# Finer steps for the gate and forget bursts of a decoder block, a step of its own for the head output's transposes, and a later wait for the last branch output

## The chip, the cores and the metric

The kernel runs on one core of a Trainium2 chip. The metric is the device time of one execution in microseconds, lower is better; times are the median of several runs.

## The reference, cut to what matters

One layer of a hybrid decoder over 256 positions of width 2048, in float32. Every weight matrix is read once.

```python
h = rmsnorm(x, g_pre_mix)
proj = h @ w_in                      # 2048 x 15376
aq, ak, av, az, ab, aa, bq, bf, bi, bz, cq, gates = split(proj)
oa = gated_head_norm(gated_deltanet(conv_silu(aq, ak, av), beta, logdecay), az)   # branch A, 8 heads of 128
log_f = logaddexp(log(lb), log1p(-lb) + log_sigmoid(bf))                          # branch B: forget gate
ob = gated_head_norm(hgrn2(silu(bq), log_f, bi), bz)                              # branch B, 8 heads of 128
oc = memory_attention(cq, rmsnorm(mem), w_kv_mem)                                 # branch C, 4 heads of 256
ga, gb, gc = split(sigmoid(gates))
merged = ga * (oa @ w_br_a) + gb * (ob @ w_br_b) + gc * (oc @ w_br_c)
x = x + rmsnorm(merged @ w_out, g_post_mix)
x = x + rmsnorm(square(relu(rmsnorm(x, g_pre_mlp) @ w1)) @ w2, g_post_mlp)        # w1: 2048 x 8192
```

Here gated_head_norm(o, z, g) is o / rms(o) * g * silu(z), per head.

## The kernel before

Every float32 product is made of three: each operand is split into a high part of a narrower type and a low part, and high x high, high x low and low x high are added in PSUM. The weights are split on the fly. A *weight group* is 256 rows x 512 columns of a matrix: one DMA on SP's queue into `w` (512 KB), a cast on ACT into `wh` (the high part), a subtraction on DVE into `wl` (the low part). `w`, `wh` and `wl` have four buffers each, so ACT and DVE can be at most four groups ahead of PE's last use.

A *unit* is one output block of 512 columns. `unit` makes 12 products of 512 columns per group (two k tiles, two row tiles, three products). `unit_joined`, for the projections whose result is wanted with channels on partitions, joins the two activation parts into one wide product (512 columns) and one narrow one (256 columns), 8 of each per group; it runs its 8 groups as pairs, and the first and the last pair in two halves of the output, so that the first half's sum can leave PSUM while the second is made. Its result goes out in two pieces, each a copy on ACT and an add on DVE (`sum<-mm`).

All other work hangs in *steps* between the groups: generators that `yield`, in the list `bg`. After each group `tick` adds the rate (R1 to R4, 1.1 to 1.2) to a credit, and `pump` runs so many steps of the first generator in the list. With `in_place` set, the first instruction of a step on DVE, ACT and PE keeps its place in the written order; the framework's scheduler may move the others by priority and readiness. Each engine then runs its queue strictly in order (PE may load weights ahead). So a step that waits at the head of ACT's or DVE's queue also holds up the casts and subtractions behind it.

The order of the program: memory attention's keys and values; the queries of C; branch A's projections (twice, four heads each), with `gen_a` as steps; branch 2 (C's gates and output); branch B's projections, twice, each time with `forget` (put ahead of all other steps) and `gen_b`; branch 0 (A's), branch 1 (B's); w_out; the MLP. A branch is four times a gate unit (sigmoid into `sg`) and an output unit of four groups, whose result times `sg` is added into `mg`.

- `forget(ps, hg)` makes log-sigmoid values of a projection: on ACT an absolute value, which waits in the place of the table switch, the table load, exp, ln (all into `fe`), then DVE and four more exps into `ft`.
- `gen_b` starts with `bm` and `bd` on DVE, then the same burst (abs, table load, exp, ln) on `bd`, then `kq`, the sum `bm + bd`, and the chunk's decay products (`ad`, `pa`, `bo` on PE).
- `head_out` is the end of `gen_a` and `gen_b`: squares on ACT, a reduction on DVE, a power on POOL (`r`), eight scalings on DVE (`on`), eight transposes on PE (`oT`), split into `oh` and `ol`.
- In `gen_a`, the triangular inverse is built by products `pw` and `pzt`, a masked copy into `XT` on DVE, and transposes `X`.

Of the kernel before, what the change touches and what calls it, by code (L numbers as in the profile page):

```python
# [33 lines left out]
KG = 2  # L34
BL = 16
WB = 4
R1, R2, R3, R4 = 1.1, 1.2, 1.2, 1.2


@with_exitstack  # L40
def tile_trunk(ctx: ExitStack, tc, a):
# [26 lines left out]
    def step_marks(begins):  # L68
        for e in (V, A, T):
            e.step_begins = begins and in_place[0]  # L70
# [14 lines left out]
    def nm(s):  # L85
        cnt[0] += 1
        return f"{s}_{cnt[0]}"

    def g4(name, shape=(P, 1024), dt=F32):
        return gp.tile(list(shape), dt, tag="g", name=nm(name))  # L90
# [5 lines left out]
    def small(name, n=16):  # L96
        if n > 16:
            return sp64.tile([P, 64], F32, tag="s64", name=nm(name))[:, 0:n]
        t = sp.tile([P, 16], F32, tag="s", name=nm(name))
        return t[:, 0:n]  # L100

    def bank(name):
        return pbp.tile([P, 512], F32, tag="bp", name=nm(name))
# [37 lines left out]
    def own_table(ins):  # L141
        other_table[0] = ins.ins
        return ins
# [10 lines left out]
    def pump(n=1):  # L154
        while n > 0 and bg:
            step_marks(True)
            try:
                next(bg[0])
                n -= 1
            except StopIteration:  # L160
                bg.pop(0)
            step_marks(False)

    def drain():
        while bg:
            pump(1)
# [12 lines left out]
    def tick(share=1.0):  # L179
        credit[0] += rate[0] * share  # L180
        n = int(credit[0])
        credit[0] -= n
        pump(n)
# [22 lines left out]
    def load_w(src, k0, n, c0, width=512, home=None):  # L206
        return split_w(load_w_raw(src, k0, n, c0, width), n, width, home=home)

    def unit(act, nk, src, c0, r0=0, order=None, split=False, post=None, ws=None):

        if split:
            ps = [bank("mm") for _ in range(2)]
        else:
            both = pmm.tile([P, 1024], F32, tag="mm", name=nm("mm"))
            ps = [both[:, 0:512], both[:, 512:1024]]
        if order is None:
            order = [(g, None) for g in range(nk // KG)]  # L220
        ws = ws or {}
        for i, (g, tt) in enumerate(order):
            k0 = g * KG
            if g not in ws:
                ws[g] = load_w(src, r0 + k0, KG, c0)
            wh, wl = ws[g]
            for j in range(KG):
                kt = k0 + j
                ah, al = act(kt)
                for t in range(NT) if tt is None else (tt,):  # L230
                    o = ps[t]
                    st, sl = ah[:, t * P:(t + 1) * P], al[:, t * P:(t + 1) * P]
                    T.matmul(o, st, wh[:, j, :], start=kt == 0, stop=False)
                    T.matmul(o, st, wl[:, j, :], start=False, stop=False)
                    T.matmul(o, sl, wh[:, j, :], start=False, stop=kt == nk - 1)
            tick()
            if post is not None and i + 1 in post:
                post[i + 1](ps)
        return ps if split else both
# [56 lines left out]
    def act_of(tiles):  # L296
        return lambda kt: (tiles[kt // 4][0][:, kt % 4, :], tiles[kt // 4][1][:, kt % 4, :])
# [9 lines left out]
    def split_psum(ps, hi, lo):  # L307
        A.copy(hi, ps)
        V.tensor_tensor(out=lo, in0=ps, in1=hi.bitcast(F32), op=ALU.subtract)
# [14 lines left out]
    def rstd_of(ss, n, count):  # L324

        v = small("v", n)
        V.tensor_scalar(out=v, in0=ss, scalar1=1.0 / count, scalar2=EPS, op0=ALU.mult, op1=ALU.add)
        r = small("r", n)
        G.tensor_tensor(out=r, in0=v, in1=mhalf[:, 0:n], op=ALU.pow)  # L329
        return r  # L330
# [409 lines left out]
    oa = [None, None]  # L740
    ob = [None, None]
# [33 lines left out]
    def head_out(o, z, rq, dst, hg):  # L775

        sq = g4("sq", (P, 8, P))
        A.activation(sq, o, AF.Square)
        ss = small("ss", 8)
        V.tensor_reduce(out=ss, in_=sq, axis=AX.X, op=ALU.add)  # L780
        yield
        if rq is not None:
            V.tensor_tensor(out=ss, in0=ss, in1=rq, op=ALU.mult)
            V.tensor_tensor(out=ss, in0=ss, in1=rq, op=ALU.mult)
        sc = rstd_of(ss, 8, P)
        if rq is not None:
            sc2 = small("sc2", 8)
            V.tensor_tensor(out=sc2, in0=sc, in1=rq, op=ALU.mult)
            sc = sc2
        on = g4("on", (P, 8, P))  # L790
        for b in range(8):
            V.scalar_tensor_tensor(out=on[:, b, :], in0=o[:, b, :], scalar=sc[:, b:b + 1], in1=z[:, b, :],
                                   op0=ALU.mult, op1=ALU.mult)
            if b % 4 == 3:
                yield
        hi, lo = g4("oh", (P, 4, S), F32R), g4("ol", (P, 4, S), F32R)
        for hh in range(2):
            pt = bank("oT")
            for q in range(2):
                for t in range(NT):  # L800
                    T.transpose(pt[:, q * S + t * P:q * S + (t + 1) * P], on[:, t * 4 + hh * 2 + q, :], ident)
            split_psum(pt.rearrange("p (q s) -> p q s", q=2), hi[:, hh * 2:hh * 2 + 2, :], lo[:, hh * 2:hh * 2 + 2, :])
        yield
        dst[hg] = (hi, lo)
# [262 lines left out]
    def gen_merge(j):  # L1067
        if j == 3:
            yield
            yield  # L1070
        hi, lo = g4("mgh", (P, 4, S), F32R), g4("mgl", (P, 4, S), F32R)
        for hh in range(2):
            pt = bank("mgT")
            for q in range(2):
                for t in range(NT):
                    c = hh * 2 + q
                    T.transpose(pt[:, q * S + t * P:q * S + (t + 1) * P], mg[j][:, t, c * P:(c + 1) * P], ident)
            split_psum(pt.rearrange("p (q s) -> p q s", q=2), hi[:, hh * 2:hh * 2 + 2, :], lo[:, hh * 2:hh * 2 + 2, :])
        mgs[j] = (hi, lo)
        yield  # L1080

    def branch(gi, o, w_br):
        oact = act_of(o)
        for j in range(4):
            ps = unit(hact, KT, w_in, OFF_G + gi * D + 512 * j)
            sg = g4("sg", (P, NT, 512))
            own_table(A.activation(sg, ps.rearrange("p (t n) -> p t n", t=NT), AF.Sigmoid))
            ps = unit(oact, 8, w_br, 512 * j).rearrange("p (t n) -> p t n", t=NT)
            if gi == 2:
                mg[j] = g4("mg", (P, NT, 512))  # L1090
                V.tensor_tensor(out=mg[j], in0=ps, in1=sg, op=ALU.mult)
            else:
                V.tensor_tensor(out=sg, in0=ps, in1=sg, op=ALU.mult)
                V.tensor_tensor(out=mg[j], in0=mg[j], in1=sg, op=ALU.add)
            if gi == 1:
                bg.append(gen_merge(j))
# [4 lines left out]
    def forget(ps, hg):  # L1101

        t, g = g4("ft", (P, 4, S)), g4("fg", (P, 4, S))

        def steps():
            e = g4("fe", (P, 4, S))
            exp_ln_table(e, ps)
            pin(A.activation(e, e, AF.Exp, scale=-1.0))
            pin(A.activation(e, e, AF.Ln, bias=1.0))
            yield  # L1110
            yield
            V.scalar_tensor_tensor(out=t, in0=ps, scalar=0.0, in1=e, op0=ALU.max, op1=ALU.add)
            yield
            for h in range(4):
                c = hg * 4 + h
                A.activation(t[:, h, :], t[:, h, :], AF.Exp, scale=-1.0, bias=lbl1[:, c:c + 1])
            V.scalar_tensor_tensor(out=g, in0=ps, scalar=0.0, in1=e, op0=ALU.min, op1=ALU.subtract)
            yield

        ahead_of_all(steps())  # L1120
        return t, g

    def gen_b(hg, k, g, q, v, z):
# [9 lines left out]
                yield  # L1133
        exp_ln_table(d, d)
        pin(A.activation(d, d, AF.Exp, scale=-1.0))
        pin(A.activation(d, d, AF.Ln, bias=1.0))
        kq, kqh, kql = g4("kq"), g4("kqdh", dt=F32R), g4("kqdl", dt=F32R)
        V.tensor_tensor(out=kq, in0=k.rearrange("p h s -> p (h s)"), in1=q.rearrange("p h s -> p (h s)"), op=ALU.mult)
# [118 lines left out]
        o = g4("ob", (P, 8, P))  # L1257
# [20 lines left out]
        bg.append(gen_b(hg, k, g, q, v, z))  # L1278
    rate[0] = R4

    while oa[1] is None:
        pump(1)
    branch(0, oa, a["w_br_a"][0])
    drain()


    def load_gbc(src):
        r = []
        for c in range(2):
            t = g4("gbc")  # L1290
            adma(t, src[0:1, c * 1024:(c + 1) * 1024].to_broadcast([P, 1024]))
            r.append(t)
        return r

    gbc = load_gbc(a["g_post_mix"])
    branch(1, ob, a["w_br_b"][0])

    def gb(c):
        return gbc[c // 2][:, c % 2 * 512:c % 2 * 512 + 512]
# [210 lines left out]
```

## Time and profile before

| what | value |
|---|---|
| median of three runs | 1805.83 us (1805.63 to 1806.97) |
| the profiled execution | 1805.44 us |
| its span, first to last instruction | 1803.7 us |
| PE busy | 1787.2 us, 99% |
| DVE busy | 1152.7 us, 64% |
| ACT busy | 901.8 us, 50% |
| mean granted PE clock | 0.997 |
| HBM read | 332.75 MB, 186 GB/s over the span |

The profile is of one execution. Its engines are PE (matmuls), PEld (PE's weight loads), DVE, ACT, POOL and SP. All instructions that go through the kernel's recording helper have line 56, so rows are told apart by the names of the tiles, output first (`wl<-w,wh`). In a timeline row the first number is the start in us, the second the length, and a bracket gives the engine's idle time before it and what ended that. The ends of matmuls are modelled; a stream of them is read by its starts.

### The profile page before, as it was taken

How to read it: one execution, taken by the hardware profiler on the slowest of the kernel's cores; microseconds unless marked ns; L12 is line 12 of the kernel's file. 1: busy time of each engine (PE TensorE's matmuls, PEld its weight loads, DVE VectorE, ACT ScalarE, POOL GpSimd, SP SyncE). 2: the span in 40 equal slices, each digit the busy share in tenths (PEclk: the TensorE clock that was granted, in tenths of full speed). 3: DMA queues.
4: the chain of work that ended last, by engine and by line, in shares of the span. 5: the costliest groups of instructions: out<-in, count | busy, mean ns of one | idle time of the engine just before them, and what ended most of it. 6: DMA issues, size and time to landing. Idle time of an engine off the chain costs nothing.

```text
span 1803.7 us, 23759 instructions
## 1 busy us (share of the span) xinstructions
PE 1787.2 (99%) x9137; PEld 1522.9 (84%) x9137; DVE 1152.7 (64%) x1599; ACT 901.8 (50%) x1148; POOL 59.7 (3%) x100
## 2 busy tenths in 40 slices
PE   9999999999999999999999999999999999999998
PEld 7888888888888888888788888888888888888886
DVE  6865768684867577696555557555655565655556
ACT  6645566454554464555444445544444444444433
POOL 0000000400120000000000000000000000000000
PEclk9999999999999999999999999999999999999999
DMA  8665545875487455555666674666666666656563
GB/s 268 204 192 166 175 148 165 240 204 151 154 214 216 122 154 175 149 187 174 189 186 186 215 235 149 191 193 192 193 187 197 192 216 187 197 184 197 187 196 136
DMA packets 176226, 336.60 MB, mean 187 GB/s; under 512 B 13656, under 2 KB 15472, under 8 KB 175728
## 3 DMA queue, kind: packets, MB, share of 16 engines
q1 hardware_dynamic: 169280, 325.10, 58.7%
q0 software_dynamic: 2304, 5.44, 1.6%
q10 hardware_dynamic: 4528, 4.54, 0.9%
q8 instruction: 71, 1.16, 0.3%
q14 instruction: 43, 0.35, 0.1%
HBM read 332.75 MB, written 2.29 MB: 186 GB/s over the span
## 4 chain that ended last, share of the span: by engine, by line
PE 83%; DVE 1%; ACT 1%; issue 0%; POOL 0%; DVEq 0%; POOLq 0%
PE mm L56 78%; PE pa L56 1%; PE kk L56 0%; PE pzt L56 0%; PE pw L56 0%; PE bo L56 0%; PE o L56 0%; DVE on L56 0%; DVE wl L56 0%; POOL r L329 0%; PE tr L56 0%; ACT L56 0%; PE y L56 0%; PE mgT L56 0%; ACT bd L56 0%
## 5 line engine op out<-in xcount | busy, mean ns | idle before, releaser
L56 DVE TENSOR_TENSOR wl<-w,wh 128x1024 fp32r<-128x1024 f32 (+1 forms) x610 | 738.3, 1219 | 523.3 <-ACT wh L56 446.9
L56 ACT CAST wh<-w 128x1024 fp32r<-128x1024 f32 (+1 forms) x610 | 636.3, 1050 | 728.3 <-PE mm L56 632.0
L56 PE MATMUL mm<-wh,hh 128*128 128x512 f32 x1152 | 366.2, 392 | 0.0
L56 PEld LDWEIGHTS mm<-wh,hh 128*128 128x128 f32 x1152 | 216.2, 188 | 44.4
L56 PE MATMUL mm<-wl,hh 128*128 128x512 f32 x576 | 224.6, 390 | 0.0
L56 PE MATMUL mm<-h2h,wh 128*128 128x512 f32 x960 | 224.4, 390 | 0.0
L56 PEld LDWEIGHTS mm<-h2h,wh 128*128 128x128 f32 x960 | 178.3, 188 | 35.8
L56 PE MATMUL mm<-wh,mh 128*128 128x512 f32 x512 | 199.2, 389 | 0.0
L56 PE MATMUL mm<-wl,mh 128*128 128x512 f32 x512 | 199.2, 389 | 0.0
L56 PE MATMUL mm<-wh,ml 128*128 128x512 f32 x512 | 199.2, 389 | 0.0
L56 PE MATMUL mm<-hh,wh 128*128 128x512 f32 x768 | 185.9, 393 | 0.8 <-ACT z L56 0.8
L56 PEld LDWEIGHTS mm<-hh,wh 128*128 128x128 f32 x768 | 141.9, 189 | 29.0 <-ACT z L56 1.0
L56 PEld LDWEIGHTS mm<-wl,hh 128*128 128x128 f32 x576 | 108.2, 188 | 21.3
L56 PEld LDWEIGHTS mm<-h2h,wl 128*128 128x128 f32 x960 | 119.3, 192 | 2.3
L56 PE MATMUL mm<-h2h,wl 128*128 128x256 f32 x960 | 120.3, 283 | 0.0
L56 PEld LDWEIGHTS mm<-wh,mh 128*128 128x128 f32 x512 | 96.1, 188 | 20.0
L56 PEld LDWEIGHTS mm<-wl,mh 128*128 128x128 f32 x512 | 96.1, 188 | 19.9
L56 PEld LDWEIGHTS mm<-wh,ml 128*128 128x128 f32 x512 | 96.1, 188 | 19.9
L56 PE MATMUL mm<-hh,wl 128*128 128x256 f32 x768 | 103.8, 287 | 2.7 <-DVE wl L56 2.7
L56 PEld LDWEIGHTS mm<-hh,wl 128*128 128x128 f32 x768 | 100.4, 194 | 6.5 <-DVE wl L56 2.9
L56 PE MATMUL mm<-wh,oh 128*128 128x512 f32 x128 | 50.2, 392 | 0.0
L56 PE MATMUL mm<-wh,mgh 128*128 128x512 f32 x128 | 50.0, 390 | 0.0
(336 smaller groups left out, 1775.4 us busy)
## 6 DMA issues: line engine op xcount, KB each, us to landing
w<-in_w_in SPq DMA_DIRECT2D x240, 512.0 KB, 4.1
w<-in_w_mlp_in SPq DMA_DIRECT2D x128, 512.0 KB, 3.9
w<-in_w_mlp_out SPq DMA_DIRECT2D x128, 512.0 KB, 4.1
w<-in_w_out SPq DMA_DIRECT2D x32, 512.0 KB, 4.4
w<-in_w_kv_mem SPq DMA_DIRECT2D x30, 512.0 KB, 5.3
w<-in_w_br_c SPq DMA_DIRECT2D x16, 512.0 KB, 3.8
w<-in_w_br_a SPq DMA_DIRECT2D x16, 512.0 KB, 4.5
w<-in_w_br_b SPq DMA_DIRECT2D x16, 512.0 KB, 4.0
```

What stands on the lines that cost most here:

```text
L56: ins = op(*args, **kwargs)
```

## The change

- `forget`: a `yield` ahead of its burst and one between exp and ln; one of the two behind ln goes.
- `gen_b`: a `yield` between the exp and the ln of its burst.
- `head_out`: a `yield` ahead of the transposes, which had shared the step of the last four scalings.
- `branch`: the wait for its input moves from ahead of branch 0 into `branch`, behind the gate unit's sigmoid; the `drain` of all steps between branch 0 and branch 1 goes.
- The load of the post-mix gain (`gbc`, two DMAs on ACT's queue) moves behind branch 1.
- The step rate R4, from branch 0 on, is 1.25 for 1.2.

```diff
@@ -34,7 +34,7 @@
 KG = 2
 BL = 16
 WB = 4
-R1, R2, R3, R4 = 1.1, 1.2, 1.2, 1.2
+R1, R2, R3, R4 = 1.1, 1.2, 1.2, 1.25
 
 
 @with_exitstack
@@ -793,6 +793,7 @@
                                    op0=ALU.mult, op1=ALU.mult)
             if b % 4 == 3:
                 yield
+        yield
         hi, lo = g4("oh", (P, 4, S), F32R), g4("ol", (P, 4, S), F32R)
         for hh in range(2):
             pt = bank("oT")
@@ -1085,6 +1086,8 @@
             ps = unit(hact, KT, w_in, OFF_G + gi * D + 512 * j)
             sg = g4("sg", (P, NT, 512))
             own_table(A.activation(sg, ps.rearrange("p (t n) -> p t n", t=NT), AF.Sigmoid))
+            while o[1] is None:
+                pump(1)
             ps = unit(oact, 8, w_br, 512 * j).rearrange("p (t n) -> p t n", t=NT)
             if gi == 2:
                 mg[j] = g4("mg", (P, NT, 512))
@@ -1103,11 +1106,12 @@
         t, g = g4("ft", (P, 4, S)), g4("fg", (P, 4, S))
 
         def steps():
+            yield
             e = g4("fe", (P, 4, S))
             exp_ln_table(e, ps)
             pin(A.activation(e, e, AF.Exp, scale=-1.0))
+            yield
             pin(A.activation(e, e, AF.Ln, bias=1.0))
-            yield
             yield
             V.scalar_tensor_tensor(out=t, in0=ps, scalar=0.0, in1=e, op0=ALU.max, op1=ALU.add)
             yield
@@ -1133,6 +1137,7 @@
                 yield
         exp_ln_table(d, d)
         pin(A.activation(d, d, AF.Exp, scale=-1.0))
+        yield
         pin(A.activation(d, d, AF.Ln, bias=1.0))
         kq, kqh, kql = g4("kq"), g4("kqdh", dt=F32R), g4("kqdl", dt=F32R)
         V.tensor_tensor(out=kq, in0=k.rearrange("p h s -> p (h s)"), in1=q.rearrange("p h s -> p (h s)"), op=ALU.mult)
@@ -1278,10 +1283,7 @@
         bg.append(gen_b(hg, k, g, q, v, z))
     rate[0] = R4
 
-    while oa[1] is None:
-        pump(1)
     branch(0, oa, a["w_br_a"][0])
-    drain()
 
 
     def load_gbc(src):
@@ -1292,8 +1294,8 @@
             r.append(t)
         return r
 
+    branch(1, ob, a["w_br_b"][0])
     gbc = load_gbc(a["g_post_mix"])
-    branch(1, ob, a["w_br_b"][0])
 
     def gb(c):
         return gbc[c // 2][:, c % 2 * 512:c % 2 * 512 + 512]
```

Three places show what this does to the engines' queues. The numbers in the names are those of the program's buffers, and differ between the two programs.

First place, ACT, at the end of the second half's forget projection (before 627 to 638 us): `sum` is that projection's way out of PSUM, `fe` its forget burst, `bd` the first half's gate burst, `wh` the casts of the next unit's weights. Before:

```order
L56 COPY sum_5724<-mm_5725 128x512
L56 ACTIVATE bd_5941<-bd_5941 128x1024
L56 ACT_TABLE_LOAD
L56 ACTIVATE bd_5941<-bd_5941 128x1024
L56 COPY sum_5724<-mm_5755 128x512
L56 ACTIVATE bd_5941<-bd_5941 128x1024
L56 ACTIVATE fe_6018<-sum_5724 128x1024
L56 ACT_TABLE_LOAD
L56 ACTIVATE fe_6018<-fe_6018 128x1024
L56 CAST wh_6042<-w_6040 128x1024
L56 ACTIVATE fe_6018<-fe_6018 128x1024
L56 CAST wh_6048<-w_6046 128x1024
```

and now:

```order
L56 COPY sum_5700<-mm_5701 128x512
L56 CAST wh_6023<-w_6021 128x1024
L56 CAST wh_6029<-w_6027 128x1024
L56 COPY sum_5700<-mm_5731 128x512
L56 CAST oh_5950<-oT_5952 128x512
L56 CAST oh_5950<-oT_5959 128x512
L56 ACTIVATE fe_6013<-sum_5700 128x1024
L56 ACT_TABLE_LOAD
L56 ACTIVATE fe_6013<-fe_6013 128x1024
L56 CAST wh_6069<-w_6067 128x1024
L56 ACTIVATE fe_6013<-fe_6013 128x1024
L56 CAST wh_6075<-w_6073 128x1024
```

Two casts stand between the two sum copies now, the `oh` casts of branch A's last head output come behind them, and the `bd` burst has left this stretch; it begins four rows behind the last of these.

Second place, DVE, at the head output of branch B's first half (before 747 to 757 us): `on` are the scalings that the transposes `oT` read, `mg` and `sg` the merge of branch 0, `ol` the low part of the transposed output. Before:

```order
L56 TENSOR_REDUCE ss_6862<-sq_6860 128x8
L56 TENSOR_TENSOR sg_6777<-mm_6779,sg_6777 128x1024
L56 TENSOR_SCALAR v_6882<-ss_6862 128x8
L56 TENSOR_TENSOR wl_6977<-w_6974,wh_6976 128x1024
L56 SCALAR_TENSOR_TENSOR on_6886<-ob_6843,r_6884,z_5722 128x128 x4
L56 TENSOR_TENSOR mg_3790<-mg_3790,sg_6777 128x1024
L56 SCALAR_TENSOR_TENSOR on_6886<-ob_6843,r_6884,z_5722 128x128 x4
L56 TENSOR_TENSOR wl_7007<-w_7004,wh_7006 128x1024
L56 TENSOR_TENSOR wl_7028<-w_7025,wh_7027 128x1024
L56 TENSOR_TENSOR ol_6935<-oT_6936,oh_6934 128x512
L56 TENSOR_TENSOR ol_6935<-oT_6943,oh_6934 128x512
```

and now:

```order
L56 TENSOR_TENSOR mg_3790<-mg_3790,sg_6756 128x1024
L56 TENSOR_TENSOR wl_6969<-w_6966,wh_6968 128x1024
L56 TENSOR_TENSOR wl_6991<-w_6988,wh_6990 128x1024
L56 TENSOR_REDUCE ss_6937<-sq_6935 128x8
L56 TENSOR_SCALAR v_6957<-ss_6937 128x8
L56 SCALAR_TENSOR_TENSOR on_6961<-ob_6900,r_6959,z_5698 128x128 x8
L56 TENSOR_TENSOR wl_7025<-w_7022,wh_7024 128x1024
L56 TENSOR_TENSOR wl_7049<-w_7046,wh_7048 128x1024
L56 TENSOR_TENSOR wl_7074<-w_7071,wh_7073 128x1024
L56 TENSOR_TENSOR wl_7100<-w_7097,wh_7099 128x1024
L56 TENSOR_TENSOR ol_7007<-oT_7008,oh_7006 128x512
L56 TENSOR_TENSOR ol_7007<-oT_7015,oh_7006 128x512
```

`mg` has left the middle of the scalings and stands ahead of the chain; four `wl` stand between the scalings and `ol`, where there were two.

Third place, ACT, at the gate burst of branch B's second half, in branch 0 (before 759 to 769 us): `sg` is the sigmoid of a gate unit, which waits for that unit's last product. Before:

```order
L56 CAST wh_7048<-w_7046 128x1024
L56 CAST wh_7074<-w_7072 128x1024
L56 ACTIVATE bd_6969<-bd_6969 128x1024
L56 ACT_TABLE_LOAD
L56 ACTIVATE bd_6969<-bd_6969 128x1024
L56 CAST kqdh_7001<-kq_7000 128x1024
L56 ACTIVATE bd_6969<-bd_6969 128x1024
L56 CAST wh_7100<-w_7098 128x1024
L56 CAST wh_7122<-w_7120 128x1024
L56 ACTIVATE qp_7092<-bm_6968 128x8x64
L56 ACTIVATE qp_7092<-bm_6968 128x8x32
L56 CAST wh_7142<-w_7140 128x1024
```

and now:

```order
L56 CAST oh_7006<-oT_7008 128x512
L56 CAST oh_7006<-oT_7015 128x512
L56 CAST wh_7120<-w_7118 128x1024
L56 ACT_TABLE_LOAD
L56 ACTIVATE sg_7068<-mm_6854 128x1024
L56 ACTIVATE bd_7041<-bd_7041 128x1024
L56 ACT_TABLE_LOAD
L56 ACTIVATE bd_7041<-bd_7041 128x1024
L56 CAST kqdh_7094<-kq_7093 128x1024
L56 ACTIVATE bd_7041<-bd_7041 128x1024
L56 CAST wh_7141<-w_7139 128x1024
```

The sigmoid and its table load stand in front of the `bd` burst now, with no cast between.

On PE, at the same place, the last of the output unit's four groups (`wh_7141`, `wl_7142`) with the first cast of the next gate unit (`wh_7170`). Now:

```order
L56 MATMUL mm_7070<-wh_7141,oh_5950 128x512
L56 MATMUL mm_7167<-wh_7170,hh_824 128x512
L56 MATMUL mm_7070<-wl_7142,oh_5950 128x512
L56 MATMUL mm_7070<-wh_7141,ol_5951 128x512
L56 MATMUL mm_7070<-wh_7141,oh_5950 128x512
```

PE reads `wl_7142` as its second product of that group, behind one product of the next unit.

## The prediction

> **What bounds the kernel now.** I read the page's first part, then who waited for whom on PE, then the timeline around the longest of those waits, then busy time and granted clock by stretch.
>
> ```profile
> span 1803.7 us, 23759 instructions
> PE 1787.2 (99%) x9137; PEld 1522.9 (84%) x9137; DVE 1152.7 (64%) x1599; ACT 901.8 (50%) x1148; POOL 59.7 (3%) x100
> ```
>
> PE is busy 99% of the span, and the matmuls are the same ones after the edit. Nothing can be won but what PE loses: time without work, and time at a lower clock. The waits that ended PE's idle time (columns: us in total, times, longest):
>
> ```profile
> PE mm L56 <- DVE wl L56: 2.7, 1, 2.7
> PE oT L56 <- DVE on L56: 2.1, 4, 1.1
> ```
>
> One wait of 2.7 us for a weight's low part, and four of 2.1 us together for head outputs' transposes. What is left of the idle time lies ahead of the point where the two programs' orders part, or behind the last product. Now the stretches of the first of these (columns after the stretch: length, then PE, PEld, DVE, ACT and POOL busy, granted clock, DMA share, GB/s):
>
> ```profile
> 636.30:638.96 2.66, 0.00 (x1) 0.00 (x1) 1.23 (x1) 2.66 (x4) 0.00 (x0) 0.90 0.00 0
> 638.96:645.30 6.34, 6.34 (x23) 5.66 (x24) 5.73 (x6) 4.19 (x7) 0.00 (x0) 0.51 0.61 167
> ```
>
> The wait has an aftermath that no wait row shows: PE is "busy" for the next 6.34 us, but at a clock of 0.51, which does the work of 3.2 us. The loss is 6.34 x 0.49 = 3.1 us, more than the wait itself. What made PE wait is in ACT's timeline:
>
> ```profile
> 627.66 0.59 ACT L56 COPY sum<-mm 128x512 f32<-128x512 f32 x1 [3.11 <-PE mm L56]
> 628.53 1.06 ACT L56 ACTIVATE bd<-bd 128x1024 f32<-128x1024 f32 x1 [0.28 <-DVE bd L56]
> 629.61 1.28 ACT L56 ACT_TABLE_LOAD   x1
> 630.90 1.06 ACT L56 ACTIVATE bd<-bd 128x1024 f32<-128x1024 f32 x1
> 631.87 0.56 ACT L56 COPY sum<-mm 128x512 f32<-128x512 f32 x1
> 632.34 1.06 ACT L56 ACTIVATE bd<-bd 128x1024 f32<-128x1024 f32 x1
> 633.29 1.05 ACT L56 ACTIVATE fe<-sum 128x1024 f32<-128x1024 f32 x1
> 634.36 1.28 ACT L56 ACT_TABLE_LOAD   x1
> 635.65 1.06 ACT L56 ACTIVATE fe<-fe 128x1024 f32<-128x1024 f32 x1
> 636.62 1.03 ACT L56 CAST wh<-w 128x1024 fp32r<-128x1024 f32 x1
> ...
> 638.96 3.97 PE L56 MATMUL mm<-hh,wl 128*128 128x256 f32 x16 [2.67 <-DVE wl L56]
> ```
>
> Two exp/ln bursts (bd of the first half of branch B, fe of the second half's forget) stand back to back between the last weight casts of one projection and the cast at 636.62. The low part (DVE, 1.2 us) follows that cast, and PE starts at 638.96.
>
> **The change part by part.**
>
> *Forget and gate bursts in steps: the gain.* In the new order (front, first place) two casts stand between the two sum copies: those of the pair of groups that PE lacked at 636.3. The bd burst comes after the fe burst, with casts between. Is the next pair late instead? After the second sum copy ACT has 0.56 for it, some 0.7 for DVE's add over half a tile that fe waits for, 1.1 for two oh casts of half a tile, fe 1.05, table 1.28, fe 1.06, cast 1.03: 6.8 us, and the cast after it 2.1 later, at 8.9. PE has 4.4 us from the same copy (631.87 to 636.3) on the first pair, then the pair now cast early: 16 wide products at the pace of these rows (start to start 0.23) and 16 narrow ones at half of it.
>
> ```profile
> 747.36 0.39 PE L56 MATMUL mm<-wl,oh 128*128 128x512 f32 x1
> 747.59 0.39 PE L56 MATMUL mm<-wh,ol 128*128 128x512 f32 x1
> ```
>
> That is 5.5 us, so the next pair is needed at 9.9 and 11.7: 3 us in hand at both. DVE's two low parts of that pair are used last there. So the 2.67 us go, and with them the 3.1 us of low clock: 5.8 us. The two programs' ACT queues differ by two table loads (31 before, 33 after); ACT is half idle, and only where such a load stands in a burst can it count (below). The forget of the first half keeps its ACT order to the row: 0.
>
> *The head output's turn as its own step.* Today the transposes are issued in the same step as the last four of the eight scalings.
>
> ```profile
> 745.96 0.59 ACT L56 COPY ob<-bo 128x512 f32<-128x512 f32 x1 [1.14 <-PE bo L56]
> ...
> 750.18 2.54 POOL L329 TENSOR_TENSOR r<-v,mhalf 128x8 f32<-128x8 f32 x1 [130.86 <-DVE v L56]
> 752.76 1.14 DVE L56 SCALAR_TENSOR_TENSOR on<-ob,r,z 128x128 f32<-128x128 f32 x4 [1.53 <-POOL r L329]
> 753.82 1.22 DVE L56 TENSOR_TENSOR mg<-mg,sg 128x1024 f32<-128x1024 f32 x1
> 754.95 1.13 DVE L56 SCALAR_TENSOR_TENSOR on<-ob,r,z 128x128 f32<-128x128 f32 x4
> 755.35 1.12 PE L56 MATMUL oT<-ident,on 128*128 128x128 f32 x7 [1.14 <-DVE on L56]
> ...
> 863.28 0.30 PE L56 MATMUL oT<-ident,on 128*128 128x128 f32 x1 [0.23 <-DVE on L56]
> 863.98 0.59 PE L56 MATMUL oT<-ident,on 128*128 128x128 f32 x3 [0.40 <-DVE on L56]
> ...
> 869.04 0.55 PE L56 MATMUL oT<-ident,on 128*128 128x128 f32 x3 [0.35 <-DVE on L56]
> ```
>
> In the new order (second place) mg is out of the scalings' way, and the transposes stand four weight groups behind the head's last product, 10.9 us, where they stood three or, at the end, two behind it. In the rows above the product had just ended at 745.96 and the last scaling at 756.1: 10.1 us with mg in it, 8.9 without. So all four waits, 2.1 us, should go. The two heads of branch A did not wait and are not moved nearer: 0.
>
> *The wait behind the gates, and the drain gone.* The old loop ahead of branch 0 finds its output there already, and issues nothing. The old drain issued the last head output (862 to 870); that is the 0.98 us at 863 and 869, counted above. In the new order the last transposes stand in the sixth of the eight gate groups of branch 1, two groups of 2.7 us before that unit ends, and their output is first read two groups into the next unit: the new loop issues nothing either. Rate 1.25 for 1.2 moves the merges' transposes by at most a group (2.7 us), behind sums that stand earlier: 0. The gain row's load:
>
> ```profile
> L56 DVE TENSOR_TENSOR y<-mm,gbc x8: 678/684/693, 1022.2 to 1092.4; 128x512 f32<-128x512 f32 x8
> L119 ACTq DMA_DIRECT2D gbc<-in_g_post_mix x2: 342/396/450, 869.6 to 870.0; - x2
> ...
> DMA to landing us min/median/max: 5.3/6.5/7.6
> ```
>
> It moves behind the last sigmoid of branch 1, about 30 us ahead of its first use at 1022, and lands in 7.6 at most: hidden.
>
> *What gets worse.* (1) The gates' sigmoid of branch 0 now falls in front of the second bd burst (front, third place). Its rows:
>
> ```profile
> L56 DVE TENSOR_TENSOR wl<-w,wh 128x1024 fp32r<-128x1024 f32 x606 | 735.5, 1223 | 522.2 <-ACT wh L56 445.8 <-PE mm L56 68.1 <-issue 5.9
> L56 ACT CAST wh<-w 128x1024 fp32r<-128x1024 f32 x606 | 633.8, 1052 | 727.1 <-PE mm L56 632.0 <-issue 53.9 <-DMA w<-in_w_in 13.6
> L56 ACT ACT_TABLE_LOAD x31 | 39.8, 1283 | 4.5 <-DVE nb L56 2.1 <-PEq L1499 1.3 <-DVE cv L56 0.6
> L56 ACT ACTIVATE sg<-mm 128x1024 f32<-128x1024 f32 x12 | 12.3, 1029 | 14.6 <-PE mm L56 14.6
> L56 ACT ACTIVATE bd<-bd 128x1024 f32<-128x1024 f32 x6 | 6.4, 1060 | 0.3 <-DVE bd L56 0.3
> L56 DVE TENSOR_TENSOR bm<-bm,bd 128x1024 f32<-128x1024 f32 x2 | 2.4, 1216 | 0.0
> ```
>
> From the gates' last product: sg 1.03, bd 1.06, table 1.28, bd 1.06, kqdh about 1.05 (a cast of that size), bd 1.06: 6.5 us; then DVE's bm 1.22 and wl 1.22, 9.0, and about 0.15 to start each side: 9.1. PE has three groups of 12 products at 0.227, 8.2 us, and two more products: 8.6. A wait of 0.5 us. Bounds: 0 if the durations overlap as they do in the rows at 633 to 637 (0.1 each), 1.3 if DVE is late by one wl more. I take 0.5. (2) The inverse's transposes X stand four products, 0.91 us, behind pzt, where they stood a whole group behind it.
>
> ```profile
> 587.33 0.48 PE L56 MATMUL mm<-wh,hh 128*128 128x512 f32 x1
> 587.56 0.74 DVE L56 COPY_PREDICATED XT<-mT,pzt 128x512 f32<-128x512 int32 x1 [3.98 <-PE pzt L56]
> ```
>
> The XT that they read is there 0.97 us after the first such product, and a start takes 0.1: a wait of 0.15 (0 to 0.5).
>
> A rule speaks against (1). The Trainium skill, "ScalarE: Activation LUTs", section "What ACT_TABLE_LOAD costs", has each table switch cost 1.28 us for the load and 1.38 for a drain. By that rule the wait would be one drain longer, an estimated 1.9 us, and the sum would come to 1800.0 where mine comes to 1798.6. The trace disagrees with the drain: the load at 629.61 begins 0.02 after its predecessor's end, and its successor starts at 630.90, as it ends.
>
> **Sum:** 2.67 + 3.1 + 2.1 - 0.5 - 0.15 = 7.2 us. The profiled execution took 1805.44 us (span 1803.7 and 1.7 around it): 1798.2. The median of the three runs lies 0.39 above it: 1798.6.
>
> **Rivals.** *A new wait that drops the clock.* A gap of 1.14 us (at 755) left the clock at full, one of 2.67 didn't. If the new wait (1), or one that I missed, lasts about as long as the old, 2.67 + 3.1 = 5.8 us come back, less the 0.5 counted: 1803.9, no difference to measure. For it: 6.5 us of ACT work without a cast stand there. Against: the old burst's rows above add up to 9.0.
>
> *The low clock isn't the gap's.* Then it stays: 1798.6 + 3.1 = 1801.7. Against: the only slow stretch inside the span begins in the only gap over 2 us, in its last fifth (a clock of 0.5 there gives the 0.90 above). In a sentence of its own, a rule would have it so: the Trainium skill, "TensorE: Matmul & The Clock Gate", Part 1, lets the clock fall after an idle window of some 3.4 us, and warns of gaps over that, and 2.67 is less. The trace disagrees as far as one case can: the fall came after a shorter gap; the low stretch, about 6.8 us, is two such windows.
>
> *DVE becomes the bound (slower).* The finer steps come at a higher rate into the stretch where DVE is fullest:
>
> ```profile
> 640.00:870.00 230.00, 227.89 (x1098) 191.88 (x1098) 178.97 (x282) 129.26 (x146) 4.18 (x2) 0.99 0.57 168
> 750.00:850.00 100.00, 98.86 (x464) 82.65 (x463) 83.32 (x140) 57.75 (x63) 2.54 (x1) 1.00 0.55 168
> ```
>
> Steps and merges are what is left of 83.3 without some 37 casts' low parts at 1.22 (45): 38 us in 100. Rate 1.25 for 1.2 adds 1.6. PE would wait for wl at every group from an addition of 16.7 on, and the kernel would be slower by 0.2% only if 7.2 + 3.6 = 11 us were short over some 150 us: 1809.4. Nothing near that is added.
>
> *The edit does nothing at 636:* another ACT burst at the same place, PE as late. The order excludes it short of a late DMA: 1804.4 (2.1 us less 0.65).
>
> **How the numbers follow.** What a measurement of this kernel can tell from no change is about 0.2%, 3.6 us. Forecast 0.70; new wait with a clock drop 0.13; clock not the gap's 0.06; nothing at 636 0.04; DVE bound 0.07. Faster: 0.70 + 0.06, and 0.04 of the new wait's 0.13, where it stays short of the full 5.8 us: 0.80. Same: the other 0.09 of it and the 0.04: 0.13. Slower: 0.07. The likeliest's own range: without the two losses 1797.9, and if the starts around the five gaps go too (about 0.15 each) 1797.2; with 1.3 and 0.5 lost 1799.8. The range for 8 in 10 takes in the clock's case and reaches up to the new wait's, and down by as much again as the starts are unsure: 1796.5 to 1804.0.
>
> **What would show it.** Right: no row of PE waiting for wl above 1 us, none for on, the granted clock at 1.00 in every stretch up to the last 30 us, an idle sum of PE some 4 us smaller. Wrong: a gap of over 2 us between 750 and 800 with mm <- wl as its row, and a clock of about 0.5 behind it; or a DVE share over 0.95 there.

## Result

| kernel | median, us | lowest to highest | runs |
|---|---|---|---|
| before | 1805.73 | 1803.52 to 1807.40 | 6 |
| changed | 1796.52 | 1795.80 to 1796.70 | 6 |

The ratio is 0.9949, 95% interval 0.9936 to 0.9962: faster by 9.2 us, where 7.2 were forecast. The median lies 0.02 us above the lower end of the stated range (1796.5 to 1804.0). Beside the last experiments both ran again: 1796.46 and 1805.18, ratio 0.9953 (0.9941 to 0.9966). The profiled execution of the changed kernel took 1795.80 us, 9.64 less than that of before.

The first part of its page:

```profile
span 1794.1 us, 23765 instructions
PE 1782.4 (99%) x9137; PEld 1520.6 (85%) x9137; DVE 1152.9 (64%) x1599; ACT 904.0 (50%) x1150; POOL 58.6 (3%) x100
```

The same matmuls are busy for 4.8 us less. Most of it, 3.1 us, is products that ran at half clock and are booked with their longer time; the rest is what the products around the waits lost (below). The whole list of PE's waits (us in total, times, longest):

```profile
PE idle L56 <- POOL ident L111: 1.6, 1, 1.6
PE mm L56 <- ACT z L56: 0.8, 1, 0.8
PE mm L56 <- DVE memT L56: 0.6, 1, 0.6
PE mm L56 <- DVE wl L56: 0.2, 1, 0.2
```

The 2.7 us for wl have become 0.2, and the line on `on` is gone. Busy time and clock by stretch (length, PE, PEld, DVE, ACT, POOL, granted clock, DMA share, GB/s), where before had clocks of 0.90 and 0.55 in the same stretches:

```profile
636.00:639.00 3.00, 3.00 (x20) 2.66 (x19) 3.00 (x4) 2.38 (x5) 0.00 (x0) 1.00 0.55 159
639.00:646.00 7.00, 7.00 (x40) 6.07 (x39) 5.39 (x11) 5.94 (x7) 0.00 (x0) 1.00 0.49 143
```

PE works through, at full clock. ACT's timeline at the same place shows how:

```profile
627.05 2.00 ACT L56 CAST wh<-w 128x1024 fp32r<-128x1024 f32 x2 [0.36 <-PE mm L56]
628.96 0.57 ACT L56 COPY sum<-mm 128x512 f32<-128x512 f32 x1
629.43 1.08 ACT L56 CAST oh<-oT 128x512 fp32r<-128x512 f32 x2
630.39 1.09 ACT L56 ACTIVATE fe<-sum 128x1024 f32<-128x1024 f32 x1
631.49 1.28 ACT L56 ACT_TABLE_LOAD   x1
632.78 1.06 ACT L56 ACTIVATE fe<-fe 128x1024 f32<-128x1024 f32 x1
633.75 1.03 ACT L56 CAST wh<-w 128x1024 fp32r<-128x1024 f32 x1
```

Two casts ahead of the second sum copy, then one burst alone. The head output's transposes and the predicted new wait, on PE:

```profile
757.78 0.39 PE L56 MATMUL mm<-wh,hh 128*128 128x512 f32 x1
758.02 1.03 PE L56 MATMUL oT<-ident,on 128*128 128x128 f32 x8
758.81 0.48 PE L56 MATMUL mm<-wh,hh 128*128 128x512 f32 x1
...
772.73 0.50 PE L56 MATMUL mm<-wh,hh 128*128 128x512 f32 x1
773.41 0.50 PE L56 MATMUL mm<-wl,oh 128*128 128x512 f32 x1 [0.18 <-DVE wl L56]
```

All eight transposes run in one go, 1.03 us from product to product. The wait at the gate burst is there, on the predicted row, with 0.18 in its bracket. By starts (0.68 from one product to the next, where the pace is 0.23) it costs 0.45.

### The profile page after: what moved, and what is told of

It reads as the page before. It is cut to its first block, busy times and chain, and to the rows that moved or that the text cites. A ratio compares the mean times of both kernels' runs of the same rounds, so it can differ in the third digit from the quotient of the medians.

```text
span 1794.1 us, 23765 instructions
## 1 busy us (share of the span) xinstructions
PE 1782.4 (99%) x9137; PEld 1520.6 (85%) x9137; DVE 1152.9 (64%) x1599; ACT 904.0 (50%) x1150; POOL 58.6 (3%) x100
## 4 chain that ended last, share of the span: by engine, by line
PE 84%; ACT 0%; DVE 0%; issue 0%; DVEq 0%; POOLq 0%; POOL 0%
PE mm L56 80%; PE pa L56 1%; PE kk L56 0%; PE pzt L56 0%; PE pw L56 0%; PE bo L56 0%; PE o L56 0%; PE tr L56 0%; PE y L56 0%; PE oT L56 0%; PE mgT L56 0%; ACT L56 0%; PE dec L56 0%; DVE x L56 0%; ACT bd L56 0%
## 5 line engine op out<-in xcount | busy, mean ns | idle before, releaser
L56 PE MATMUL mm<-wl,oh 128*128 128x512 f32 x128 | 50.0, 390 | 0.2 <-DVE wl L56 0.2
```

The source lines that it names most:

```text
L56: ins = op(*args, **kwargs)
```

## Experiments

Times are medians, and gains are against the runs of before on the same chip (1804.74, 1804.56, 1805.18 or 1805.14).

### The parts alone

**Bursts alone:** the `yield`s in `forget` and `gen_b`.

```diff
         def steps():
+            yield
             e = g4("fe", (P, 4, S))
...
             pin(A.activation(e, e, AF.Exp, scale=-1.0))
+            yield
             pin(A.activation(e, e, AF.Ln, bias=1.0))
-            yield
             yield
...
         pin(A.activation(d, d, AF.Exp, scale=-1.0))
+        yield
         pin(A.activation(d, d, AF.Ln, bias=1.0))
```

> Only the two bursts are cut into steps (forget and gen_b); the head output, the wait, the drain, the gain's load and the rate are as before. Theory (each loss has its own price, and they add up): the wait of 2.67 us at 636 and the low clock behind it go, 5.8 to 6.3 us; at the head output of branch B's first half mg no longer stands between the scalings, so of its 1.14 us at most a half stays; the waits for on at the drain (863 to 870, 0.98 us in their rows) stay. 1805.7 - 6.0 - 0.7 = 1799.0, between 1798 and 1800.5, and the clock at 1.00 everywhere ahead of the last product. Rival 1 (the clock drop isn't the gap's): the wait goes and a stretch of 6.8 us at a clock of 0.5 stays somewhere inside the span, 1802. Rival 2 (the head output's step and the removed drain bring the gain, the bursts little): 1803 or more.

Measured: 1799.40, ratio 0.9970 (0.9958 to 0.9981), a gain of 5.3. The wait at 636 and its low clock are gone, and so is the wait for `on` at 755. What stays is PE's wait at the drain, now in one piece:

```profile
PE oT L56 <- DVE on L56: 1.7, 1, 1.7
```

**Head output alone:** one `yield` ahead of the transposes.

```diff
             if b % 4 == 3:
                 yield
+        yield
         hi, lo = g4("oh", (P, 4, S), F32R), g4("ol", (P, 4, S), F32R)
```

> Only the head output's transposes get a step of their own; the bursts are not cut, and everything behind is as before. The added step (one for each of the two heads of branch A) moves all later steps back by about one weight group each, and in the order two casts then stand between the two sum copies at the end of the second half's forget projection, as in the changed kernel. Theory (what counts at 636 is where the two bursts fall against the unit's end, not their being cut): the 2.67 us and the low clock go, 5.8 to 6.3 us, the wait of 1.14 us for on at 755 goes too, the waits at the drain (0.98 us in their rows) stay or are shorter: 1805.7 - 6.0 - 1.2 = 1798.5, between 1797.5 and 1800. Rival (a burst must be cut, or it holds up the casts): a wait for wl of 2 us or more stays between 630 and 645, with or without the low clock, and the time is 1801.5 to 1804.5.

Measured: 1799.19, ratio 0.9969 (0.9958 to 0.9980), a gain of 5.5. No burst is cut, and the 636 us wait is gone all the same: the rival that a burst must be cut falls. The added steps of branch A's two heads move all later steps back, and so the bursts out of each other's way: the bd burst, which began at 628.5 before, begins at 638.9, behind fe's. The drain's wait stays:

```profile
PE oT L56 <- DVE on L56: 1.8, 1, 1.8
```

**The rest alone:** the moved wait, no drain, `load_gbc` behind branch 1, rate 1.25.

```diff
-R1, R2, R3, R4 = 1.1, 1.2, 1.2, 1.2
+R1, R2, R3, R4 = 1.1, 1.2, 1.2, 1.25
...
             own_table(A.activation(sg, ps.rearrange("p (t n) -> p t n", t=NT), AF.Sigmoid))
+            while o[1] is None:
+                pump(1)
...
-    while oa[1] is None:
-        pump(1)
     branch(0, oa, a["w_br_a"][0])
-    drain()
...
+    branch(1, ob, a["w_br_b"][0])
     gbc = load_gbc(a["g_post_mix"])
-    branch(1, ob, a["w_br_b"][0])
```

> Only the wait moved into branch, the drain gone, the gain's load behind branch 1 and the rate 1.25 for 1.2; bursts and head output as before. Theory: the order at 636 is that of the kernel before, so the wait of 2.67 us and the low clock stay; the waits for on at the drain (0.98 us in their rows, perhaps 1.9 with what their starts lose) go, and mg is out of the scalings at 755 (1.14 us, of which some or all goes): 1805.7 - 2.5 = 1803.2, between 1802.5 and 1804.8. Rival 1 (the drain and the wait are most of the gain): 1800 or less. Rival 2 (they are worth nothing alone, because the transposes still share a step with the last scalings): 1805 to 1806, with waits for on of 1 us or more.

Measured: 1802.20, ratio 0.9986 (0.9977 to 0.9994), a gain of 2.5, just under the interval forecast. The wait at 636 stays, and none for `on` is left:

```profile
PE mm L56 <- DVE wl L56: 3.0, 2, 2.7
```

The clock behind it was at half for 3.41 us in this trace, where before it was 6.83:

```profile
638.92:642.33 3.41, 3.40 (x16) 3.10 (x16) 3.04 (x3) 2.87 (x5) 0.00 (x0) 0.50 0.74 168
```

**`gen_b`'s `yield` alone**, the last hunk of the bursts.

> Only gen_b's burst is cut between its exp and its ln. The order then has one cast between the first burst's exp and its ln at 630 to 637, and the forget's burst still follows before the casts that PE lacks: by the rows of before I get a wait for wl of about 1.9 us in place of 2.67, between 1.0 and 2.4. Theory A (the clock falls after a gap of this length): 1.9 + 3.1 us stay of 5.8, the rest gains about 0.8 and the mg out of the scalings at 755 about 0.7, 1804.2. Theory B (the clock falls only past some length between 1.14 and 2.67 us, or only when the gap lies badly in the window in which PE's use is counted): the clock stays at 1.00, 1805.7 - 0.8 - 3.1 - 0.7 = 1801.1.

Measured: 1801.31, ratio 0.9980 (0.9971 to 0.9989), with runs from 1799.86 to 1802.69. The traced one took 1802.58 and had, as expected, a shorter wait:

```profile
PE oT L56 <- DVE on L56: 1.8, 1, 1.8
PE mm L56 <- DVE wl L56: 1.7, 1, 1.7
```

Behind the 1.73 us at 637.90 the clock fell for 3.42 us; behind the 1.78 at 863.31 it stayed up. So neither theory holds as written: it isn't the length alone. The runs differ, too. Six of the eleven have a mean clock of 0.999, which leaves room for 5.4 us at half clock; the low stretch at the end of the span alone takes 3.3 to 6.3 in the traces, so a window of 3.41 doesn't fit. Their median is 1800.5. The other five, the traced one among them, stand at 0.998, with a median of 1802.5.

### Parts together

**Bursts and head output, without the rest.**

> Bursts and the head output in steps; the moved wait, the removed drain, the gain's load and the rate left as before. Theory (one cause at 636, which either of the two edits removes; the drain is a loss of its own): no better than the bursts alone or the head output alone, which took 1799.4 and 1799.2: 1799.0, between 1798.3 and 1799.9, with one wait of PE for on of about 1.75 us at 860 and the clock at 1.00 up to the last product. Rival (the two edits add up): 5 us more, 1794.

Measured: 1798.66, ratio 0.9967 (0.9955 to 0.9979), a gain of 5.9 where 5.3 and 5.5 would add up to 10.8. Both edits remove the same losses, the one at 636 and the wait for `on` at 755. The drain's wait is as predicted:

```profile
PE oT L56 <- DVE on L56: 1.7, 1, 1.7
```

**Head output and the rest, bursts uncut.**

> The head output in a step of its own and the moved wait, the removed drain, the gain's load and the rate; the bursts are not cut. Theory (the cutting of the bursts is worth nothing beside the shift of the later steps): as the changed kernel, 1796.5 to 1797.5, without a wait for wl above 1 us at 636 and with at most half a microsecond of waits between 750 and 880. Rival (cut bursts matter once the drain is gone, since the uncut burst meets other work): 1 us or more above the changed kernel, with a wait for wl that its trace shows.

Measured: 1797.93, ratio 0.9964 (0.9952 to 0.9977). The time is above the theory's range and in the rival's, 1.4 us above the changed kernel at rate 1.2 on the same chip (1796.49, below), and the wait for wl that the rival asks for is there. So here the rival holds: at 636 the bursts need not be cut, but left whole they cost elsewhere. Two waits of its list are not in the changed kernel's at this size:

```profile
PE mm L56 <- DVE sum L56: 0.9, 1, 0.9
PE mm L56 <- ACT z L56: 0.8, 1, 0.8
PE mm L56 <- DVE wl L56: 0.8, 1, 0.8
```

The first (549.6) is the first half's projection, whose sum is held up on DVE by a step of branch A's inverse; the third (772.8) stands on ACT behind the sigmoid, its two table loads and a decay step (`qp`) of branch B's second half, which had the uncut bd burst ahead of them (762.55 to 765.50). In the changed kernel that wait is 0.2.

**The changed kernel at rate 1.2.**

> The changed kernel with the rate back at 1.2. Theory (the rate moves steps by at most a group and prices nothing): 1796.5, within 0.8 of the changed kernel. Rival (the higher rate is needed to bring the last transposes in before their output is read): a new wait of PE for on at 865 to 875, and 1 us or more.

Measured: 1796.49, ratio 0.9957 (0.9944 to 0.9969): the rate prices nothing. Against bursts and head output alone, on the same chip, the moved wait, the drain and the gain's load bring 2.2 us; the row that goes is the drain's 1.74.

### The collision put back

In the changed kernel the two casts of the next pair are made to wait for the forget's burst, with one extra pass over `fe` (an absolute value of what is already positive).

```diff
     def load_w(src, k0, n, c0, width=512, home=None):
+        if home is None and behind[0] > 0:
+            behind[0] -= 1
+            w = load_w_raw(src, k0, n, c0, width)
+            with tc.issue_after(behind[1]):
+                return split_w(w, n, width)
...
             exp_ln_table(e, ps)
+            for _ in range(1 * hg):
+                pad = pin(A.activation(e, e, AF.Abs))
+                behind[:] = [2, pad.ins]
             pin(A.activation(e, e, AF.Exp, scale=-1.0))
```

`hg` is 1 for the second half alone, so the first half's forget gets no pass.

> The changed kernel with one thing put back: the two casts of the next unit's first pair stand behind the forget's burst again (abs, table load, one extra pass over fe, then the casts between exp and ln). By the rows of before: 0.56 for the sum copy, about 0.9 for two oh casts and DVE's add, 1.05 + 1.28 + 1.06 + 1.03 on ACT, 1.22 for the low part, 7.1 us after a copy behind which PE has 4.4: a wait for wl of 2.7 us, between 2.3 and 3.3. Theory (the late pair and the low clock that it brings are two thirds of the whole gain): 1796.5 + 2.7 + 1.7 for one window of 3.413 us at half clock, or 3.4 for two: 1800.9 or 1802.6, between 1800 and 1803.5. Rival (the pair was late only because two bursts stood in its way, and one burst costs nothing): 1796.5 to 1797.5.

Measured: 1798.07, ratio 0.9961 (0.9949 to 0.9974), 1.6 us above the changed kernel beside it (1796.46). It lies between both expectations, and the clock stayed up. PE's timeline:

```profile
634.47 1.11 PE L56 MATMUL mm<-hh,wl 128*128 128x256 f32 x8
636.31 1.21 PE L56 MATMUL mm<-hh,wl 128*128 128x256 f32 x8 [0.73 <-DVE wl L56]
638.21 1.21 PE L56 MATMUL mm<-hh,wl 128*128 128x256 f32 x8 [0.68 <-DVE wl L56]
```

ACT's side was right: the sum copy began at 629.17, and the low part was there at 636.3, 7.1 us later. PE's side was not: it had work up to 635.58, 6.4 us behind the copy and not 4.4. In the kernel before, the copy itself had been late. Its last product had run out by about 630.3 (PE's rows: eight narrow products from 629.28, the next unit's from 630.29), but it stood behind bd's burst up to 631.87. So the first burst took 1.6 us before the second took its own.

**Three passes for one.**

> As the run with the late pair, with three extra passes over fe in place of one, so the pair's casts come 2.12 us later. That run's trace has waits of 0.73 and 0.68 us and no window at half clock, at 1798.07. Here the first becomes 2.85 and the second stays: 3.5 us of idle time, 0.2 for the starts. Theory (a wait of that size in one or two windows costs a window at half clock besides): 1796.5 + 3.7 + 1.7 = 1801.9, between 1801.4 and 1802.5, or 1803.6 if two windows run at half clock as in the profiled execution of before, and the trace has a stretch of 3.41 or 6.83 us at 0.5 that begins at a multiple of 3.413 us from the first rise. Rival (at this place the clock stays up, and the wait alone counts): 1800.2.

Measured: 1801.92, ratio 0.9985 (0.9976 to 0.9994), runs from 1800.66 to 1804.45: 5.5 us above 1796.46 (before stood at 1805.14 on this chip and at 1805.18 on that one). The theory's place and size hold, its count doesn't: the profiled execution, at 1802.26, has one wait of 2.91 and two windows at half clock. No second wait follows: the 16 narrow products behind it ran for 3.8 us at half clock, and the next low part was there in time.

```profile
637.93:644.76 6.83, 6.23 (x22) 5.63 (x23) 6.16 (x6) 5.63 (x9) 0.00 (x0) 0.50 0.66 174
```

### What a gap does to the clock

Twelve hold-ups in the changed kernel's MLP: extra passes over a scratch tile, behind which the next five casts are issued.

```diff
+    def hold_up(n):
...
+        first = tc.issue_after(last_cast[0])
+        with first:
+            d = A.activation(pad, pad, AF.Abs)
+        for _ in range(n - 1):
+            with tc.issue_after(d.ins):
+                d = A.activation(pad, pad, AF.Abs)
+        behind[0], behind[1] = 5, d.ins
```

> The changed kernel with twelve hold-ups in the MLP: at the second group of an output unit the casts wait behind 8, 9, 10 or 11 extra passes of ACT over a scratch tile of 128x1024 (in this order, three times), so that PE runs out of weights. By 1.05 a pass and about 7.5 us that ACT can be late, PE is idle for about 0.9, 1.95, 3.0 and 4.05 us, 30 us in all. Theory A (PE's use is counted in windows of 3.413 us that run on by themselves, and a window that is more than about half idle is followed by one at half clock, each costing 1.7 us): no drop behind the gaps of 0.9, a drop behind about half of those of 1.95, behind nearly all of 3.0 and 4.05, each beginning at a multiple of 3.413 us from the first rise of the clock: 30 + 14 to 19, 1841 to 1846. Theory B (the length of the gap alone decides, with a threshold between 1.14 and 1.73 us): every gap from 1.95 on is followed by a drop at once, wherever it lies. Theory C (the clock needs a gap of 3.4 us or more): only the last kind, 1832.

Measured: 1842.07, ratio 1.0210 (1.0196 to 1.0224). The sizes came out in two kinds, since a cast of the MLP's own stood among the passes at every other place (`mh` at 1264.03, 1.04 us): six stalls of about 1.4 us (0.61 and 0.76, or 0.90 and 0.53, half a microsecond of products between), six of about 3.6 (2.79 and 0.76, 3.07 and 0.49). None of the first is followed by a drop, each of the others by one of 3.413 us. In the trace's clock records all drops begin at a whole number of 3.4133 us from the first rise, 399.00, 407.00, 455.00 and so on; so do the one of before, 185.00, and that of the rest alone, 185.00. Theory C falls: no single gap reached 3.4 us. That the time lies in theory A's range is partly luck. Six drops are some 10 us, fewer than it counted; the starts around the stalls lost some 5 us more, which it didn't count (1842.07 less 1796.5, less 29.9 of idle time).

**Twelve nearly equal stalls.** 9 passes at the one place of each round and 10 at the other.

> The changed kernel with twelve hold-ups as in the run with gaps, but nearly equal ones: 9 passes at the second and 10 at the fourth output unit of six rounds. By that run's rows (0.61 us of idle for 8 passes, 2.79 for 10; 0.90 for 9, 3.07 for 11, and a second wait of 0.76 or 0.53 half a microsecond later) PE is idle for 1.7 + 0.76 or 1.98 + 0.53 us each, 29.8 in all, and each stall costs 0.47 more in starts: 1832 without a drop. Theory A (windows of 3.413 us running on by themselves, threshold near half of one): equal gaps fare differently by where they lie in their window; about 7 of 12 are followed by one window at half clock, those whose idle time falls mostly into one window, and each costs 1.7: 1844, between 1840 and 1849. Theory B (the length alone decides): all twelve, 1852, or none, 1832.

Measured: 1843.62, ratio 1.0215 (1.0201 to 1.0229); 1844 was expected. In the trace seven of the twelve are followed by a drop: four of the six with a first gap of 1.70 us, three of the six with 1.98. Two stalls of the same size, 1.70 and 0.76 us, a window's view each (the gap, up to the next whole multiple, and the window behind):

```profile
1369.16:1370.86 1.70, 0.01 (x1) 0.00 (x0) 0.01 (x1) 1.70 (x3) 0.00 (x0) 1.00 0.00 0
1370.86:1373.67 2.81, 2.04 (x8) 1.45 (x9) 2.81 (x3) 2.81 (x3) 0.00 (x0) 1.00 0.14 37
1373.67:1377.08 3.41, 3.41 (x17) 2.81 (x16) 1.81 (x2) 1.03 (x1) 0.00 (x0) 1.00 0.89 286
1560.60:1562.30 1.70, 0.00 (x0) 0.00 (x0) 0.02 (x1) 1.70 (x3) 0.00 (x0) 1.00 0.00 0
1562.30:1564.82 2.52, 1.76 (x6) 1.24 (x7) 2.52 (x3) 2.52 (x3) 0.00 (x0) 1.00 0.06 20
1564.82:1568.23 3.41, 3.41 (x9) 2.63 (x8) 2.09 (x2) 0.85 (x2) 0.00 (x0) 0.50 0.88 290
```

The first stall is cut by a multiple (1370.26) so that the fuller of its two windows was idle for 40%; the second's (cut at 1561.41) was idle for 48%: no drop and a drop, 17 products against 9 in the window behind. Over all twelve, with the modelled ends of matmuls, windows idle for 48% to 72% led to a drop and those for 40% to 50% did not. The length alone (theory B) falls.

## Why the prediction was right, and where it was off

What was to show it right is there: no wait for wl above 1 us, none for `on`, the clock at 1.00 up to the last product, and 4.9 us less idle time ahead of PE's products (8.05 before, 3.17 after, all gaps added). The sum was 2.1 us short, though: 1796.52 lies 0.7 below the range given for the likeliest case (1797.2 to 1799.8) and just inside the wide one, and the second set's 1796.46 just outside. The mechanism was right; that the number fell inside is luck. What was too small is told term by term.

**The wait of 2.67 us** went, as said, and so did the low clock of the profiled execution: 6.27 us of products in 6.83 at 0.50, 3.1 us lost, as forecast. With what the starts around it lose, the place gives 6.3 of the 9.64 us (each matmul's time to the next start, less the median of its form, summed from 550 to 650: 7.65 before, 1.36 after).

**The working for the next pair** (needed at 9.9 and 11.7, 3 us in hand) rested on 4.4 us of work behind the sum copy. That was a copy delayed by bd's burst; PE has 2 us more. No harm to the forecast, since the error lay on the safe side, but it failed as a number in the run with the late pair.

**The clock's 3.1 us** is the profiled execution's price, not the kernel's. The traces show one window or two, 1.7 or 3.4 us, and in the run of `gen_b` alone some runs had none. That bears on the sum, which set one execution's loss against the median of all. Most of before's runs paid: of the 58 whose mean clock is on record, 37 stand at 0.997, which is 9.0 us or more at half clock, where the end of the span takes 6.3 at most. One, at 0.999, had no such window (1803.00); the 20 at 0.998 may have had one or none. This lottery alone doesn't give the spread of before's times: on one chip 17 runs at 0.997, with a window or two, go from 1802.76 to 1807.42, and a window is worth 1.7. What else spreads them is open.

**The oT waits, 2.1 us,** are the mis-sized term: 3.2. I took the idle time in the brackets; the products' starts say more. At 755 it is 2.51 us from the product ahead (753.71) to the one behind (756.22), where now it is 1.03: 1.5, for the 1.14 booked. At the drain it is 1.90 (862.42 to 864.32) and 1.04 (868.30 to 869.34), against 1.03 and an ordinary step of 0.23: 1.7, for the 0.98 booked. So each bracket understates its wait, by 0.3 us in the one at 755 and by 0.7 in the three at the drain.

**The new wait, 0.5,** came on its row with 0.45 by starts. The Trainium skill, "ScalarE: Activation LUTs", section "What ACT_TABLE_LOAD costs", would have made it 1.9 with a drain per load, by the prediction's estimate. The trace disagrees again: in the changed kernel's first burst shown, the first `fe` pass ends at 631.48, the load begins at 631.49, and exp starts at 632.78, 1.29 later. **The X transposes, 0.15:** no wait is to be seen. **Rate, `gbc`, the moved wait at branch 0, branch A's heads: 0,** which the run at 1.2 shows for the rate; the others have no wait in the changed kernel's list.

Summed by starts: 6.3 + 3.2 - 0.45, and 0.44 less in the first 50 us, where the code is the same and the traces here differ by up to 1 us: 9.5 of the 9.64.

**The rivals.** A new wait that drops the clock: the wait came, with 0.18 us of idle time, far below any that dropped the clock here. DVE as the bound: it was busy for 84.1 us of the 100 from 750 to 850, where it was 83.3. Nothing at 636: that wait is gone. The low clock not the gap's: the drop went with the gap, and came back with it in the run with three passes. There the Trainium skill, "TensorE: Matmul & The Clock Gate", Part 1, has a free-running window of 3413 ns; the clock records agree to 0.01 of a window. It also has the clock fall after an idle window of that length; the trace disagrees, since windows that were 48% idle sufficed.

**The cause as the plan told it** needs one correction. The cure at 636 needs no finer step: the head output's `yield`, which cuts no burst, did it alone. Steps are issued by count, and any added step moves all later ones. The 636 loss was two bursts that happened to meet at the end of a unit. In the run of the bursts alone, which also cured it, the cut and the shift were not told apart. Cutting is worth 1.4 us beside the other edits, by the run with uncut bursts, at other places.

## To carry to other kernels

Where steps are dealt out by count, read a change first as a shift of all later steps, and look in the order for what now stands next to what; whether the edit itself matters, the other edit alone tells. Price a gap on PE by the starts around it and not by its bracket, and add the price of a clock window, 1.7 us, if it may idle about half of one: no window at full clock that idled for less than 48% was followed by a low one here. Before adding the gains of two edits, ask if they remove the same wait.

## What the hardware showed

A drop starts at the next multiple of 3.4133 us after the window that was idle, not with the gap: in the second stall above 1.26 us of products ran at full clock first (1563.56 to 1564.82), and two stalls equal to 0.01 us can cost 1.7 us more or less. Open: why the low stretch was two windows in before and in the run with three passes, and one everywhere else. In the first two the gap reached 0.16 and 0.17 of a window into the next, with narrow products behind it; gaps that reached in by 0.14 and 0.15 with wide products behind gave one window. No run separates the two. Open too is the gap of 1.78 us ahead of transposes in the run of `gen_b` alone, 52% of its window, with no drop, where 51% at 637.90 had one: the limit is known only to lie about half a window (48% to 52%), as the ends of matmuls are modelled.
